# Scores of 64-wide heads in an encoder trunk: two products over 128 rows, then two over 64 rows each

## The chip, the cores and the metric

The kernel runs on one core of a Trainium2 chip. A core has TensorE (PE; its weight loads are listed apart as PEld), VectorE (DVE), ScalarE (ACT), GpSimd (POOL) and SyncE (SP), which issues most DMAs. The metric is the device time of one execution in microseconds.

## What is computed

Two layers of a bidirectional encoder over 1024 tokens of width 1024. In each layer one input projection feeds three kinds of attention, whose outputs are concatenated, projected and added; then comes a gated feed-forward. Cut to the attention scores:

```python
# MLA: 6 heads, 96 wide, 64-wide values
o_a = _dense_attention(q_a, k_a, v_a, MLA_QK ** -0.5, "bhqd,bhsd->bhqs", "bhqs,bhsv->bhqv")
# differential: 4 heads of two 64-wide score maps each
s = jnp.einsum("bhcqd,bhcsd->bhcqs", qb, k_b).astype(jnp.float32) * scale_b
p = jax.nn.softmax(s, axis=-1)
a = p[:, :, 0] - lam * p[:, :, 1]
# grouped-query: 6 query heads, 2 key heads, 64 wide
o_c = _dense_attention(q_c, k_c, v_c, GQA_DIM ** -0.5, "bkgqd,bksd->bkgqs", "bkgqs,bksv->bkgqv")
```

So a layer has 8 + 6 = 14 score maps of 64-wide heads and 6 of 96-wide heads, each of 1024 queries by 1024 keys.

## The kernel before

Every operand of a large product is held as two parts, a high one (the value rounded to fp32r) and a low one (what the rounding left). A product is then the sum of high by low, low by high and high by high. The parts of queries and keys are written to DRAM once (`qd`, `kd` for differential heads, `qg`, `kg` for grouped-query heads, `qm`, `km` for MLA), with the features along the rows, and read back by head.

The attention stage handles 320 calls of `soft` over both layers: 20 score maps, 8 blocks of 128 queries, 2 layers. One call makes the scores of 128 queries against all 1024 keys in a PSUM tile `sc` of two banks, 512 keys ("half") in each; VectorE takes the maximum over the tile (L688) and ScalarE the exponential (L689). The tile has two buffers. Then the probabilities are transposed on PE (`spread`, L704), split into high and low (L709, L710) and multiplied with the values (L890).

For a 64-wide head both parts of one operand fit on the 128 rows of a tile. `load_q` makes two query tiles, `q[0]` with high over low and `q[1]` with low over high. `load_k` makes one key tile for each half of the keys, `k[0]` and `k[1]`, both with high over low. Then `q[1]` by a key tile is low by high plus high by low, and `q[0]` by it is high by high plus low by low: two products of 128 rows for each half, four for a call. The 96-wide heads need three products for each half, six for a call.

What sets the order: `order` mixes the streams of units (five of single heads to two of differential ones), `front`, `one_spread` and `value_products` lay the work of several units between each other, and queries and keys are loaded two blocks of 256 queries ahead. The instructions are placed by a scheduler that works from a time line of its own, so that SP's row of DMAs can shift when PE's work changes.

`neg_lambda` (L179) has one small matmul of 64 rows in each layer, and the finish of a differential head has small ones of 128 rows (L811).

Of the kernel before, what the change touches and what calls it, by code (L numbers as in the profile page):

```python
# [20 lines left out]
P = 128  # L21
# [44 lines left out]
def encoder(ctx: ExitStack, tc: tile.TileContext, a: dict, out: bass.AP):  # L66
    nc = tc.nc
    ve, ac, po, pe, sy = nc.vector, nc.scalar, nc.gpsimd, nc.tensor, nc.sync
# [14 lines left out]
    def ps_s(name):  # L83
        return banks["pool"].tile([P, 2, 512], F32, tag="s", name=name)
# [12 lines left out]
    def ps_u(name):  # L97
        return banks["pool"].tile([P, 512], F32, tag="u", name=name)

    def ps_v(name):  # L100
        return banks["pool"].tile([P, 512], F32, tag="v", name=name, bufs=5)
# [94 lines left out]
    for l in range(L):  # L196
# [78 lines left out]
        def gain_row(name):  # L275
# [11 lines left out]
            lambda k, tt, i=i: XT[tt // 4][i][:, k, tt % 4 * P : (tt % 4 + 1) * P] for i in range(2)  # L287
# [343 lines left out]
        with tc.tile_pool(name=f"c{l}", bufs=2, side=there, reuse_waits="tile") as cp:  # L631
            QB = 256
            n = QB // P
            def stacked(t, parts, rows, cols):
                for r, src in enumerate(parts):
                    sy.dma_start(out=f(t[r * rows : (r + 1) * rows, :]), in_=src[:, cols])
                return t[: rows * len(parts)]

            def load_k(k, rows, tag):

                out = []
                for i in range(2):
                    orders = [[k[0], k[1]]] if 2 * rows <= P else [[k[0]], [k[1]]]
                    out.append(
                        [
                            stacked(
                                ops.tile([P, 512], F32R, tag=tag, name="k"), o, rows,
                                slice(i * 512, (i + 1) * 512),
                            )
                            for o in orders  # L650
                        ]
                    )
                return out
# [21 lines left out]
            def soft(q, k, i):  # L675
                ps = ps_s("sc")
                cut = slice(i * P, (i + 1) * P)
                for half, kk in enumerate(k):
                    products = ((1, 0), (0, 1), (0, 0)) if len(kk) == 2 else ((1, 0), (0, 0))
                    for at, (x, y) in enumerate(products):  # L680
                        pe.matmul(  # L681
                            ps[:, half, :], q[x][:, cut], kk[y], start=at == 0, stop=at == len(products) - 1
                        )
                nm = cp.tile([P, 1], F32, tag="nm", name="nm", bufs=6)
                s = cp.tile([P, 1], F32, tag="sum", name="sum", bufs=8)
                p = cp.tile([P, S], F32, tag="p", name="p", bufs=7)
                pf = ps.rearrange("p a b -> p (a b)")
                ve.tensor_reduce(nm, pf, axis=AX.X, op=ALU.max, negate=True)  # L688
                ac.activation(p, pf, AF.Exp, bias=nm, accum_out=s)  # L689
                return p, s  # L690
# [34 lines left out]
            class Single:  # L725
# [8 lines left out]
                def load(self):  # L734
                    self.kk = load_k(self.k, self.rows, "b")
                    (self.vv,) = v_tiles(self.v, "b", 2)
# [4 lines left out]
                def front(self, b, i):  # L741
                    p, s = soft(b.q, self.kk, i)
                    r = recip(s)
                    po.tensor_scalar(p, p, r, 1.0, ALU.mult, ALU.mult)  # L744
                    yield p
# [14 lines left out]
            class Diff:  # L760
# [5 lines left out]
                def load(self):  # L766
                    self.kk = [
                        load_k([kd[p, i] for p in range(2)], DD, "a") for i in (2 * self.h, 2 * self.h + 1)
                    ]
                    self.vv = [  # L770
                        t[:, k * 2 * P : (k + 1) * 2 * P].rearrange("p (c x) -> p c x", c=2)
                        for t in v_tiles(vd[self.h], "a", 3)
                        for k in range(TT // 2)
                    ]
# [7 lines left out]
                def front(self, b, i):  # L782

                    if i == 0:
                        b.es = cp.tile([P, QB // P], F32, tag="es", name="es")
                    p0, s0 = soft(b.q[0], self.kk[0], i)
                    yield None
                    p1, s1 = soft(b.q[1], self.kk[1], i)
                    r1 = recip(s1)
                    c = cp.tile([P, 1], F32, tag="c", name="c", bufs=6)  # L790
                    po.tensor_scalar(c, s0, nlam, 1.0, ALU.mult, ALU.mult)
                    po.tensor_scalar(b.es[:, i : i + 1], s0, s0, EPS, ALU.mult, ALU.mult)
                    po.tensor_scalar(p1, p1, c, r1, ALU.mult, ALU.mult)
                    po.tensor_tensor(out=p0, in0=p0, in1=p1, op=ALU.add)
                    yield p0
# [70 lines left out]
            fronts, lagging, spreads, products, ends = [], [], [], [], []  # L866
# [30 lines left out]
            at = 0  # L897
# [85 lines left out]
        for tt in range(TT):  # L983
            ps = ps_u("psd") if tt % 2 else ps_v("psd")
# [48 lines left out]
        for tt in range(TT):  # L1033
# [5 lines left out]
            ps = ps_u("psd") if tt % 2 else ps_v("psd")  # L1039
# [204 lines left out]
        at = 0  # L1244
        w_d = a["w_down"][l].rearrange("(n two p) d -> two p n d", two=2, p=P)
        for p0 in range(0, NP, NC):
# [49 lines left out]
            for step, (an, bn, bank, start, (row, c)) in enumerate(steps):  # L1296
# [7 lines left out]
                for tt in range(TT // 2):  # L1304
                    if start:
                        acc[bank, tt] = ps_u("psy") if bank == "c" and tt < 3 else ps_v("psy")
                    ps = acc[bank, tt]
# [3 lines left out]
                    x = XQ[row][c][:, tt, :]  # L1311
# [39 lines left out]
```

## Time and profile before

| | |
|---|---|
| median of 3 runs | 3335.84 us (3328.43 to 3336.86) |
| profiled execution | 3334.67 us |
| its span, first to last instruction | 3332.9 us |
| mean granted TensorE clock | 0.974 |
| scores L681: matmuls, first and last start | 1472, at 401.9 and 2535.9 us |
| maximum L688 on VectorE | 320 of 1213 ns |
| exponential L689 on ScalarE | 320 of 1120 ns |

The time of an execution is its span and what lies around it. Matmuls are pipelined: a matmul's listed duration includes a tail that lies under the next one, so that what a matmul costs is read from start to start. The busy shares are averages over stages with different limits; the attention stages are two of them, from about 401 to 880 us and from 2056 to 2540 us.

### The profile page before, as it was taken

What the parts mean: (1) busy time and instruction counts of PE and PEld (TensorE: products, weight loads), DVE (VectorE), ACT (ScalarE), POOL (GpSimd) and SP (SyncE); (2) the same over time, 40 slices, a digit from 0 to 9 for tenths busy, and PEclk for the clock granted to TensorE, in tenths of its full rate; (3) what the DMA queues carried; (4) which work ended last, traced back from release to release, by engine and by line L of the source; (5) the groups of instructions that cost most, each with busy time, mean ns of one, the idle gap of its engine ahead of it and who ended that gap; (6) DMA issues with size and microseconds to landing.
All of it is one profiled execution on the core that took longest, in us unless ns stands there. A gap on an engine that the chain in (4) does not pass through costs nothing.

```text
span 3332.9 us, 50137 instructions
## 1 busy us (share of the span) xinstructions
PE 3112.6 (93%) x17628; PEld 2725.3 (82%) x17628; DVE 2412.0 (72%) x4880; ACT 1589.5 (48%) x3010; POOL 1067.6 (32%) x1178
## 2 busy tenths in 40 slices
PE   8888899999898999989998888999898989999899
PEld 7888888888787888878898888888787878888787
DVE  5876688999637665667669776999995376666776
ACT  4433377777624333333344344777774243333332
POOL 1634466666302100100026344666663020101000
PEclk9999899999999999999998999999999999999999
DMA  5565634333572333374344665433336723334632
GB/s 150 158 197 164 192 100 118 109 97 98 166 260 81 101 114 95 101 258 152 98 138 144 187 189 177 117 106 111 90 102 205 233 79 95 101 108 142 230 133 98
DMA packets 386075, 466.16 MB, mean 140 GB/s; under 512 B 36768, under 2 KB 275360, under 8 KB 385824
## 3 DMA queue, kind: packets, MB, share of 16 engines
q1 hardware_dynamic: 372416, 418.38, 40.6%
q0 software_dynamic: 13408, 44.57, 4.0%
q8 instruction: 140, 2.29, 0.3%
q14 instruction: 111, 0.91, 0.1%
HBM read 313.42 MB, written 149.42 MB: 139 GB/s over the span
## 4 chain that ended last, share of the span: by engine, by line
PE 69%; DVE 19%; DMA 5%; issue 2%; ACT 2%; POOL 1%; SPq 1%; ACTq 0%; DVEq 0%; POOLq 0%
PE pv L890 6%; PE sc L681 6%; PE psa L157 5%; PE psa L158 5%; PE psa L159 5%; PE ptc L704 4%; PE psb L157 4%; PE psb L158 4%; PE psb L159 4%; PE psy L157 4%; PE psy L159 4%; PE psy L158 4%; DVE nm L688 4%; DVE pl L710 3%; PE psc L157 2%
## 5 line engine op out<-in xcount | busy, mean ns | idle before, releaser
L681 PE MATMUL sc<-k,q 128*128 128x512 f32 (+1 forms) x1472 | 421.5, 414 | 23.7 <-ACT p L689 23.0
L157 PE MATMUL psb<-wh,xl 128*128 128x256 f32 (+2 forms) x1280 | 389.2, 305 | 38.8 <-DVE vst L431 20.2
L688 DVE TENSOR_REDUCE nm<-sc 128x1 f32<-128x1024 f32 x320 | 388.1, 1213 | 46.3 <-PE sc L681 44.7
L689 ACT ACTIVATE p<-sc,nm 128x1024 f32<-128x1024 f32 x320 | 358.5, 1120 | 81.2 <-DVE nm L688 71.4
L158 PE MATMUL psb<-wl,xh 128*128 128x256 f32 (+2 forms) x1280 | 386.8, 302 | 2.7 <-POOL wl L124 2.2
L159 PE MATMUL psb<-wh,xh 128*128 128x256 f32 (+2 forms) x1280 | 385.2, 301 | 0.0
L710 DVE TENSOR_TENSOR pl<-ptc,ph 128x512 fp32r<-128x512 f32 x512 | 337.5, 677 | 14.1 <-ACT ph L709 13.3
L709 ACT CAST ph<-ptc 128x512 fp32r<-128x512 f32 x512 | 288.8, 586 | 105.7 <-PE ptc L704 99.9
L681 PEld LDWEIGHTS sc<-k,q 128*128 128x128 f32 (+1 forms) x1472 | 260.0, 192 | 70.1 <-ACT p L689 30.3
L890 PE MATMUL pv<-pl,v 128*128 128x256 f32 x1024 | 277.8, 296 | 39.2 <-DVE pl L710 27.7
L704 PE MATMUL ptc<-ident,p 128*128 128x128 f32 x2048 | 290.5, 276 | 19.1 <-DVE pl L710 15.5
L890 PE MATMUL pv<-ph,v 128*128 128x256 f32 x1280 | 304.3, 288 | 2.8 <-DVE ot L756 2.4
L157 PEld LDWEIGHTS psb<-wh,xl 128*128 128x128 f32 x1280 | 250.5, 196 | 43.0 <-issue 13.6
L704 PEld LDWEIGHTS ptc<-ident,p 128*128 128x128 f32 x2048 | 242.1, 143 | 52.6 <-DVE pl L710 10.3
L744 POOL TENSOR_SCALAR p<-p,rec 128x1024 f32<-128x1024 f32 x192 | 216.1, 1128 | 136.3 <-DVE rec L694 99.1
L157 PE MATMUL psy<-bh,al 128*128 128x512 f32 x616 | 241.9, 396 | 16.6 <-DVE al L124 16.6
L158 PEld LDWEIGHTS psb<-wl,xh 128*128 128x128 f32 x1280 | 251.1, 196 | 3.8 <-POOL wl L124 2.8
L1222 POOL DMA_DIRECT2D hd<-h x66 | 35.9, 545 | 681.0 <-DVE h L1163 434.3
L159 PEld LDWEIGHTS psb<-wh,xh 128*128 128x128 f32 x1280 | 250.3, 196 | 0.0
L158 PE MATMUL psy<-bl,ah 128*128 128x512 f32 x616 | 241.7, 392 | 0.1
L890 PEld LDWEIGHTS pv<-pl,v 128*128 128x128 f32 x1024 | 195.4, 191 | 56.0 <-DVE pl L710 37.4
L159 PE MATMUL psy<-bh,ah 128*128 128x512 f32 x616 | 241.2, 392 | 0.0
(220 smaller groups left out, 7656.2 us busy)
## 6 DMA issues: line engine op xcount, KB each, us to landing
graw<-in_w_gate_up SPq DMA_DIRECT2D x88, 512.0 KB, 5.3
ar<-hd SPq DMA_DIRECT2D x28, 1024.0 KB, 6.1
hd<-hs POOLq DMA_DIRECT2D x88, 256.0 KB, 3.0
hd<-h POOLq DMA_DIRECT2D x66, 256.0 KB, 2.4
q<-qd SPq DMA_DIRECT2D x256, 64.0 KB, 2.4
B<-od SPq DMA_DIRECT2D x12, 1280.0 KB, 7.6
wraw<-in_w_in SPq DMA_DIRECT2D x56, 256.0 KB, 3.2
o<-od SPq DMA_DIRECT2D x10, 1280.0 KB, 11.2
```

The lines of the kernel that those rows point to most:

```text
L157: pe.matmul(ps, xl, wh, start=first, stop=False, skip_group_check=more)
L158: pe.matmul(ps, xh, wl, start=False, stop=False, skip_group_check=more)
L159: pe.matmul(ps, xh, wh, start=False, stop=last, skip_group_check=more)
L681: pe.matmul(ps[:, half, :], q[x][:, cut], kk[y], start=at == 0, stop=at == len(products) - 1)
L688: ve.tensor_reduce(nm, pf, axis=AX.X, op=ALU.max, negate=True)
L689: ac.activation(p, pf, AF.Exp, bias=nm, accum_out=s)
L704: pe.transpose(pt[:, k * P : (k + 1) * P], p[:, (4 * b + k) * P : (4 * b + k + 1) * P], ident)
L709: ac.copy(h, pv)
L710: ve.tensor_tensor(out=pl[:, 4 * b : 4 * b + 4, i * P : (i + 1) * P], in0=pv, in1=f(h), op=ALU.subtract,)
L744: po.tensor_scalar(p, p, r, 1.0, ALU.mult, ALU.mult)
L890: pe.matmul(b.o, x, y, start=first, stop=last)
L1222: po.dma_start(out=HB[b][p], in_=src)
```

## The change

It concerns 64-wide heads alone. The key tile of the second half is now stacked with low over high. The first product of the first half is still `q[1]` by `k[0]` (low by high plus high by low); that of the second half becomes `q[0]` by `k[1]` (high by low plus low by high). Both run over all 128 rows. Then only high by high is left. For the first half it lies on rows 0 to 63 of `q[0]` and `k[0]`, for the second on rows 64 to 127 of `q[1]` and `k[1]`, and each is a product of 64 rows. The low by low product, which the 128-row form brought along for these heads, is no longer computed. The order of the four products becomes: first half, second half, first half, second half.

```diff
             def load_k(k, rows, tag):
 
+
                 out = []
                 for i in range(2):
-                    orders = [[k[0], k[1]]] if 2 * rows <= P else [[k[0]], [k[1]]]
+                    orders = [[k[i], k[1 - i]]] if 2 * rows <= P else [[k[0]], [k[1]]]
...
-                for half, kk in enumerate(k):
-                    products = ((1, 0), (0, 1), (0, 0)) if len(kk) == 2 else ((1, 0), (0, 0))
-                    for at, (x, y) in enumerate(products):
-                        pe.matmul(
-                            ps[:, half, :], q[x][:, cut], kk[y], start=at == 0, stop=at == len(products) - 1
-                        )
+                if len(k[0]) == 1:
+
+
+                    for half, (kk,) in enumerate(k):
+                        pe.matmul(ps[:, half, :], q[1 - half][:, cut], kk, start=True, stop=False)
+                    for half, (kk,) in enumerate(k):
+                        rows = slice(half * 64, half * 64 + 64)
+                        pe.matmul(ps[:, half, :], q[half][rows, cut], kk[rows], start=False, stop=True)
+                else:
+                    for half, kk in enumerate(k):
+                        products = ((1, 0), (0, 1), (0, 0))
+                        for at, (x, y) in enumerate(products):
+                            pe.matmul(ps[:, half, :], q[x][:, cut], kk[y], start=at == 0, stop=at == 2)
```

PE's order in layer 0, well inside the attention stage: transposes of probabilities (`ptc`), scores of a 64-wide head, transposes, scores of a 96-wide head, values (`pv`). Before:

```order
L704 MATMUL ptc<-ident,p 128x128 x4
L681 MATMUL sc<-k,q 128x512 x4
L704 MATMUL ptc<-ident,p 128x128 x8
L681 MATMUL sc<-k,q 128x512 x6
L890 MATMUL pv<-ph,v 128x256 x2
```

The same place in the changed kernel, whose lines stand two to eight further down:

```order
L712 MATMUL ptc<-ident,p 128x128 x4
L683 MATMUL sc<-k,q 128x512 x2
L686 MATMUL sc<-k,q 128x512 x2
L712 MATMUL ptc<-ident,p 128x128 x8
L691 MATMUL sc<-k,q 128x512 x6
L898 MATMUL pv<-ph,v 128x256 x2
```

The four score products have become two of 128 rows (L683) and, right behind, two of 64 rows (L686); the row shows the output's size, which is the same. The 96-wide head's six and all around them stand where they stood.

PE's order at the start of the first attention stage, with the semaphores that an instruction waits for (those named DMA are loads of queries and keys, DVE and Activation the release of a PSUM buffer). Before:

```order
L681 MATMUL sc<-k,q 128x512 [waits DMAHW5_49,DMAHW4_49,DMAHW7_49,DMAHW0_49,DVE_49]
L681 MATMUL sc<-k,q 128x512 [waits DMAHW6_49]
L681 MATMUL sc<-k,q 128x512 [waits DMAHW1_49,DMAHW0_49]
L681 MATMUL sc<-k,q 128x512
L681 MATMUL sc<-k,q 128x512 [waits DMAHW3_49,DMAHW2_49,DVE_49]
```

In the changed kernel:

```order
L683 MATMUL sc<-k,q 128x512 [waits DMAHW5_49,DMAHW4_49,DMAHW7_49,DMAHW0_49,DVE_49]
L683 MATMUL sc<-k,q 128x512 [waits DMAHW6_49,DMAHW1_49,DMAHW0_49]
L686 MATMUL sc<-k,q 128x512 x2
L683 MATMUL sc<-k,q 128x512 [waits DMAHW3_49,DMAHW2_49,DVE_49]
L683 MATMUL sc<-k,q 128x512 [waits DMAHW2_49]
```

The loads of the second key tile are waited for by the second product of a call instead of the third; the two products of 64 rows wait for nothing of their own.

SP's order in layer 0 where it differs: loads of queries (`q<-qd`, `q<-qm`) and keys (`k<-kd`) and stores of outputs (`od<-ohl`). Before:

```order
L636 DMA k<-kd 64x512
L636 DMA q<-qd 64x256 x6
L720 DMA od<-ohl 128x2x256
L636 DMA q<-qd 64x256 x2
L720 DMA od<-ohl 64x2x256
L671 DMA v<-vm 128x1024
L636 DMA q<-qm 96x256 x2
L636 DMA k<-kd 64x512 x7
```

In the changed kernel:

```order
L636 DMA q<-qd 64x256 x7
L728 DMA od<-ohl 128x2x256
L636 DMA q<-qd 64x256
L728 DMA od<-ohl 64x2x256
L672 DMA v<-vm 128x1024
L636 DMA q<-qm 96x256 x2
L636 DMA k<-kd 64x512 x8
```

One load of keys has moved behind the queries ahead of it. VectorE's, ScalarE's and GpSimd's rows are the same in both kernels but for line numbers.

## The prediction

> **What bounds the kernel now.** I read the page first, then the two stretches in which scores are computed, then the chain of waits inside them, then single instructions. The page, with the span, the engines and the chain that ended last:
>
> ```profile
> span 3332.9 us, 50137 instructions
> PE 3112.6 (93%) x17628; PEld 2725.3 (82%) x17628; DVE 2412.0 (72%) x4880; ACT 1589.5 (48%) x3010; POOL 1067.6 (32%) x1178
> PE 69%; DVE 19%; DMA 5%; issue 2%; ACT 2%; POOL 1%; SPq 1%; ACTq 0%; DVEq 0%; POOLq 0%
> ```
>
> PE carries the kernel as a whole, but the change touches only the attention stage of each layer. The first scores of layer 0 start at 401 us, the last of layer 1 at 2536 us; the two stages as windows (columns: engine busy times, PE clock, DMA share, GB/s):
>
> ```profile
> core 0: us, PE busy (x) PEld busy (x) DVE busy (x) ACT busy (x) POOL busy (x), PEclk, DMA share, GB/s
> 401.00:880.00 479.00, 442.57 (x2908) 391.40 (x2907) 428.22 (x802) 357.58 (x702) 291.62 (x314) 0.98 0.39 115
> 2056.00:2540.00 484.00, 443.62 (x2934) 391.41 (x2932) 434.09 (x812) 363.68 (x714) 293.79 (x316) 0.99 0.40 116
> ```
>
> PE is busy 92% of such a stage and VectorE 89%. So there are two engines near their limits, and a microsecond on PE is worth less than a microsecond at the end. How much less is read from the chain of work inside each window, and from who waits:
>
> ```profile
> by line: PE sc L681 22.1%; PE pv L890 21.6%; PE ptc L704 13.1%; DVE nm L688 13.0%; DVE pl L710 10.0%; DVE t L137 3.2%; DVE r L138 2.6%; DVE t L136 2.1%; ACT p L689 1.8%; issue 1.7%; DMA raw<-in_w_o 1.3%; DVE ot L756 1.2%; PE pb L827 1.0%; D
> by line: PE sc L681 21.4%; PE pv L890 20.8%; PE ptc L704 13.2%; DVE nm L688 12.6%; DVE pl L710 9.9%; DVE t L137 3.2%; DVE r L138 2.5%; issue 2.4%; ACT p L689 2.3%; DVE t L136 2.1%; DMA raw<-in_w_o 1.4%; DVE ot L756 1.2%; ACT ph L709 1.0%; P
> ...
> DVE nm L688 <- PE sc L681: 23.9, 32, 2.6
> PEld pv L890 <- DVE pl L710: 18.8, 18, 2.7
> PEld sc L681 <- ACT p L689: 14.3, 13, 4.1
> ```
>
> The score products (L681) hold 22.1% of 479 us and 21.4% of 484 us, 106 + 104 = 210 us, of both chains. In layer 0 VectorE stands 23.9 us for scores, and PE stands for VectorE and ScalarE about as long. Neither engine has the stage to itself.
>
> **What a block of scores costs now.** A block is one call of `soft`: 128 queries against 1024 keys. For 64-wide heads it is four products of 128 rows by 512 columns. The counts by shape, and one block with the instructions around it (start, length of the group):
>
> ```profile
> L681 PE MATMUL sc<-k,q 128*128 128x512 f32 x896 | 265.3, 419 | 17.6 <-ACT p L689 17.3
> ...
> 708.98 0.28 PE L890 MATMUL pv<-ph,v 128*128 128x256 f32 x1
> 709.10 1.09 PE L681 MATMUL sc<-k,q 128*128 128x512 f32 x4
> 710.03 0.49 PE L704 MATMUL ptc<-ident,p 128*128 128x128 f32 x3
> ```
>
> The listed mean of 419 ns includes the tail of a pipelined matmul; what counts is start to start: 710.03 - 709.10 = 0.93 us for four, 0.2325 us each. 896 / 4 = 224 blocks are changed; the other 96 blocks, of the 96-row heads, have six products each (320 blocks in all) and stay. All score products take (896 + 576) x 0.2325 = 342 us, of which 210 us lie on the chain: 0.61. That is the share of a saved score microsecond that reaches the end; for a lengthening it is the lower bound, 1.0 the upper.
>
> **What the change removes.** Two of the four 128-row products become two 64-row products, on rows 0-63 and 64-127, each with 512 columns and into its own PSUM bank. If these two run side by side they take one slot instead of two: -0.2325 us a block, 224 x 0.2325 = -52 us on PE. The number of matmuls and weight loads stays; only their rows fall.
>
> **What it adds.** Each block now goes from 128-row to 64-row matmuls and back. The trace of before has exactly two such visits, one in each layer: L179, two small matmuls with 64 rows in the middle of a stream of 128-row products. PE rows of the first and its weight loads, then the second:
>
> ```profile
> 65.78 0.28 PE L159 MATMUL psb<-wh,xh 128*128 128x256 f32 x1
> 65.90 0.28 PE L157 MATMUL psb<-wh,xl 128*128 128x256 f32 x1
> 66.11 0.38 PE L179 MATMUL pl__5271<-lp,ones 64*128 64x2 f32 x2
> 66.42 0.38 PE L158 MATMUL psb<-wl,xh 128*128 128x256 f32 x1
> 66.64 0.28 PE L159 MATMUL psb<-wh,xh 128*128 128x256 f32 x1
> ...
> 65.66 0.19 PEld L159 LDWEIGHTS psb<-wh,xh 128*128 128x128 f32 x1
> 65.78 0.19 PEld L157 LDWEIGHTS psb<-wh,xl 128*128 128x128 f32 x1
> 66.10 0.29 PEld L179 LDWEIGHTS pl__5271<-lp,ones 64*128 64x128 f32 x2
> 66.41 0.19 PEld L158 LDWEIGHTS psb<-wl,xh 128*128 128x128 f32 x1
> ...
> 1725.31 0.28 PE L157 MATMUL psb<-wh,xl 128*128 128x256 f32 x1
> 1725.52 0.38 PE L179 MATMUL pl__22793<-lp,ones 64*128 64x2 f32 x2
> 1725.83 0.39 PE L158 MATMUL psb<-wl,xh 128*128 128x256 f32 x1
> 1726.05 0.28 PE L159 MATMUL psb<-wh,xh 128*128 128x256 f32 x1
> ```
>
> In the plain stream a load stands one matmul ahead (the load at 65.78 belongs to the matmul at 65.90). Around L179 that stops: its load starts at 66.10, 0.01 us ahead of its own matmul, and so does the next load back, at 66.41. Both layers give the same gaps within 0.01 us and the profile names no wait there, so I read it as the price of the visit and not of late data. For comparison, two equally small matmuls of all 128 rows (L811):
>
> ```profile
> 706.26 0.28 PE L890 MATMUL pv<-ph,v 128*128 128x256 f32 x1
> 706.38 0.28 PE L811 MATMUL pm<-ones,osq 128*128 128x1 f32 x2
> 706.52 1.19 PE L681 MATMUL sc<-k,q 128*128 128x512 f32 x4
> 707.54 0.28 PE L811 MATMUL pm<-ones,osq 128*128 128x1 f32 x2
> ...
> 706.26 0.31 PEld L811 LDWEIGHTS pm<-ones,osq 128*128 128x128 f32 x2
> 706.49 0.77 PEld L681 LDWEIGHTS sc<-k,q 128*128 128x128 f32 x4
> ```
>
> Here the loads run ahead as always. The visit's price, term by term:
> - going in: 66.11 - 65.90 = 0.21 us instead of 706.38 - 706.26 = 0.12: +0.09
> - the pair and going out: 66.42 - 66.11 = 0.31 us instead of 706.52 - 706.38 = 0.14: +0.17
> - the first full product after it, whose load lies open: 66.64 - 66.42 = 0.22 us instead of 0.12: +0.10. After L811 the four scores take 707.54 - 706.52 = 1.02 us instead of 0.93, +0.09 as well, so this term may belong to the small pair and not to the change of rows.
>
> So a visit costs 0.26 us without the last term and 0.36 us with it. I take 0.36: before, the load behind a block was hidden, and after it the row of L179 shows it open. There is one more unknown: whether the loads of the two halves go beside each other. Two loads of L179 take 0.29 us where one takes 0.19, so a second load can put the second half 0.10 us behind the first; L179's two share their rows, the new pair doesn't, so I count it at nothing and keep 0.10 us for the upper end.
>
> **The sum.** Per block 0.36 - 0.2325 = +0.13 us (bounds: 0.26 - 0.2325 = +0.03 and 0.46 - 0.2325 = +0.23). Times 224: +29 us of PE time (+7 to +51). The end gets 0.61 to 1.0 of it; PE grows into more of the chain as it slows, but its present waits for VectorE absorb some, so I take 0.8: +23 us. On the profiled execution's 3334.67 us (its span of 3332.9 and 1.8 around it; the median of the runs is 3335.84) this is **3358 us**; this case's own range is 3334.67 + 0.61 x 7 = 3339 to 3334.67 + 51 = 3386.
>
> On this place the Trainium skill speaks against the change: TensorEngine Tiling (Array Packing), section Key Properties, says that a change of the tiling mode, as opposed to a change of tile within it, drains the TensorE. The trace agrees, with the 0.20 us from the last full matmul's start at 65.90 to the load at 66.10.
>
> **What costs nothing.** The second key tile is now stacked low over high. It is loaded by the same DMAs, and a handful of them change places by a row or two in SP's queue:
>
> ```profile
> q<-qd SPq DMA_DIRECT2D x256, 64.0 KB, 2.4
> k<-kd SPq DMA_DIRECT2D x64, 128.0 KB, 3.7
> ```
>
> They are issued two blocks of 256 queries ahead, that is at least four units of a stage that takes 479 / 160 = 3 us a unit of `soft`; 12 us cover 3.7. Were that cover gone, each of the 28 loads of keys could cost its 3.7 us, but none of PE's waits above is for keys. Each half's first product now comes second in the block instead of third, so the second tile is wanted 0.23 us earlier, well inside the same cover. VectorE, ScalarE and GpSimd keep their instructions and order. No wait is added; the reduction behind a block (L688) sees both halves end together instead of one after the other, but it waited for the last of them before too.
>
> **Rivals.**
> 1. *The pair is side by side and the visit is nearly free* (faster). The pause around L179 would then belong to its small plain-float matmuls and not to 64 rows. All of -52 us is saved on PE, 0.61 of it at the end: -32 us, 3303 us. VectorE allows it: its 428 us of a 479 us stage leave 51 us. It decides wherever a visit costs under 0.2325 us a block. For it: only two visits are on record, both with two columns. Against it: L811 is as small and as plain and shows no pause going in.
>    In the Trainium skill, TensorE: Matmul & The Clock Gate, section Measured speedup vs the span model, counts packed row tiles as one matmul and about 4 ns for each further tile. By that rule a block is three slots, which is this rival; no run here shows a packed pair yet.
> 2. *The two halves don't overlap* (slower still). A block keeps four slots and pays 0.26 to 0.36 us: 58 to 81 us on PE, at 0.8 46 to 65 us, 3381 to 3399 us. For it: no matmul in this trace overlaps another by more than its tail. Against it: different rows and different PSUM banks. This is also the case that the change doesn't do what its words say.
> 3. *It cancels.* A visit of 0.19 to 0.27 us eats the saved slot, within about 0.04 us x 224 = 9 us: 3335 us, give or take 9.
>
> **How the numbers follow.** Forecast 0.45, rival 1 0.24, rival 2 0.12, rival 3 0.19. A measurement of this kernel can tell about 0.3%, 10 us, from no change. Slower: 0.42 of the forecast, 0.12, and 0.02 of rival 3, together 0.56. Within: 0.03 of the forecast, 0.02 of rival 1, 0.15 of rival 3, 0.20. Faster: 0.22 of rival 1 and 0.02 of rival 3, 0.24. The range from 3308 to 3392 leaves out the far end of rival 1 (about 0.1) and the upper half of rival 2 (0.06); the likeliest case alone spans 3339 to 3386.
>
> **What would show it.** In the profile after, the load of the first 64-row product should start about 0.3 us (a 0.21 us stream and 0.09) behind the start of the last 128-row one and not beside it; the two 64-row matmuls should start within 0.1 us of each other; from a block's first product to the next instruction should be 1.0 to 1.1 us instead of 0.93, and each stage some 11 us longer. If the 64-row loads stand ahead as the others do, rival 1 is right; if the second half starts 0.23 us behind the first, rival 2. The forecast is also wrong if blocks lengthen as worked out but the stages don't: then PE's waits for VectorE took it up.

## The result, and the profile after

The changed kernel takes 3354.70 us in the median of 5 runs (3350.54 to 3357.92), the kernel before 3335.84 us (3328.43 to 3339.32). The ratio is 1.0056, with a 95% interval from 1.0041 to 1.0072: slower by about 19 us. The forecast was 3358 us.

The page of the changed kernel; its profiled execution took 3357.92 us, the longest of the five:

```profile
span 3356.1 us, 50132 instructions
PE 3146.6 (94%) x17628; PEld 2673.6 (80%) x17628; DVE 2417.7 (72%) x4880; ACT 1593.2 (47%) x3010; POOL 1069.6 (32%) x1178
PE 72%; DVE 17%; DMA 5%; ACT 2%; issue 2%; SPq 1%; POOL 0%; ACTq 0%; DVEq 0%; POOLq 0%
```

PE has 34 us more of busy time with the same 17628 matmuls, and its share of the chain that ended last rose from 69% to 72%, at VectorE's cost. Where the time lies is seen from the first score and the last transpose of each layer. The answers by line, for layer 0 and layer 1 (duration in ns as min/median/max, then first and last start in us); first the kernel before:

```profile
L681 PE MATMUL sc<-k,q x736: 387/395/794, 401.9 to 882.2; 128*128 128x512 f32 x112, 96*128 96x512 f32 x72
L704 PE MATMUL ptc<-ident,p x1024: 270/272/421, 411.1 to 894.9; 128*128 128x128 f32 x171
...
L681 PE MATMUL sc<-k,q x736: 387/394/792, 2056.6 to 2535.9; 128*128 128x512 f32 x112, 96*128 96x512 f32 x72
L704 PE MATMUL ptc<-ident,p x1024: 270/272/448, 2067.4 to 2548.6; 128*128 128x128 f32 x171
```

The same of the changed kernel (its transposes are L712):

```profile
L683 PE MATMUL sc<-k,q x224: 387/397/795, 398.6 to 856.3; 128*128 128x512 f32 x112
L712 PE MATMUL ptc<-ident,p x1024: 270/273/477, 407.9 to 903.2; 128*128 128x128 f32 x171
...
L683 PE MATMUL sc<-k,q x224: 387/398/796, 2063.1 to 2524.0; 128*128 128x512 f32 x112
L712 PE MATMUL ptc<-ident,p x1024: 270/273/472, 2074.0 to 2571.8; 128*128 128x128 f32 x171
```

From the first score to the last transpose, layer 0 takes 903.2 - 398.6 = 504.6 us instead of 493.0, layer 1 508.7 instead of 492.0: +28 us together. The stage of layer 0 begins 3 us earlier and the stretch between the stages is 2 us shorter; behind the last transpose both kernels take 784.3 us. All of the loss is in the two attention stages.

The granted clock of these stages is lower too. It is TensorE's clock as a share of its full speed, here a mix of stretches at 1 and at 0.5; at 0.5 a score matmul is listed with up to 796 ns where the median is 398. The two stages of the changed kernel as windows (columns as in the prediction, the clock third from the end):

```profile
401.00:880.00 479.00, 446.00 (x2835) 354.93 (x2836) 422.52 (x788) 351.72 (x689) 286.11 (x308) 0.97 0.38 112
2056.00:2540.00 484.00, 452.48 (x2874) 358.80 (x2873) 420.38 (x782) 350.04 (x686) 282.88 (x304) 0.97 0.40 115
```

The kernel before had 0.98 and 0.99. Over the whole span the mean of the five runs is 0.972, against 0.976 in the eleven runs of the kernel before beside the first experiments: an estimate of 0.004 x 3355 = 13 us less of full clock.

One block of the changed kernel, at the place that the prediction showed of before (PE, then its weight loads; start and length of the group):

```profile
709.72 0.28 PE L898 MATMUL pv<-ph,v 128*128 128x256 f32 x1
709.84 0.63 PE L683 MATMUL sc<-k,q 128*128 128x512 f32 x2
710.40 0.50 PE L686 MATMUL sc<-k,q 64*128 64x512 f32 x2
710.82 0.66 PE L712 MATMUL ptc<-ident,p 128*128 128x128 f32 x4
711.32 0.60 PE L835 MATMUL pb<-dg,ones 128*128 128x256 f32 x2
...
709.72 0.31 PEld L683 LDWEIGHTS sc<-k,q 128*128 128x128 f32 x2
710.39 0.18 PEld L686 LDWEIGHTS sc<-k,q 64*128 64x128 f32 x2 [0.37 <-issue]
```

Three things are to be seen. The two 64-row matmuls, 0.494 us each by their median, take 0.50 us together, so they start together and do run side by side. Their two loads take 0.18 us together, where two loads into the same rows took 0.29: the loads go side by side too. But the load starts at 710.39, 0.55 us behind the first full product, instead of ahead of its matmul: PE's loads stood idle for 0.37 us, and the profile names nobody ("issue") as the one waited for.

The same over all blocks: the 64-row matmuls' durations, then groups by shape (count, then busy time and mean, then idle time just before):

```profile
L686 PE MATMUL sc<-k,q x448: 491/494/794, 399.1 to 2524.3; 64*128 64x512 f32 x150
...
L683 PE MATMUL sc<-k,q 128*128 128x512 f32 x448 | 161.1, 442 | 15.3 <-ACT p L697 15.3
L686 PE MATMUL sc<-k,q 64*128 64x512 f32 x448 | 114.8, 509 | 0.0
L686 PEld LDWEIGHTS sc<-k,q 64*128 64x128 f32 x448 | 42.7, 187 | 85.0 <-issue 85.0
```

224 pairs have 85.0 us of such idle time ahead of their loads, 0.38 us each. A matmul of 0.509 us mean is listed 448 times, but its busy time is 114.8 us, 0.51 for each pair: half of them lie beside the other half everywhere.

### The profile page after: what moved, and what is told of

Its sections match the earlier page's. It is cut to its first block, busy times and chain, and to the rows that moved or that the text cites. A ratio compares the mean times of both kernels' runs of the same rounds, so it can differ in the third digit from the quotient of the medians.

```text
span 3356.1 us, 50132 instructions
## 1 busy us (share of the span) xinstructions
PE 3146.6 (94%) x17628; PEld 2673.6 (80%) x17628; DVE 2417.7 (72%) x4880; ACT 1593.2 (47%) x3010; POOL 1069.6 (32%) x1178
## 4 chain that ended last, share of the span: by engine, by line
PE 72%; DVE 17%; DMA 5%; ACT 2%; issue 2%; SPq 1%; POOL 0%; ACTq 0%; DVEq 0%; POOLq 0%
PE pv L898 7%; PE psa L157 5%; PE psa L158 5%; PE psa L159 5%; PE ptc L712 5%; PE psb L157 4%; PE psb L158 4%; PE psb L159 4%; PE psy L157 4%; PE psy L159 4%; PE psy L158 4%; DVE nm L696 3%; DVE pl L718 3%; PE sc L691 3%; PE psc L157 2%; PE psc L158 2%
## 5 line engine op out<-in xcount | busy, mean ns | idle before, releaser
L898 PE MATMUL pv<-pl,v 128*128 128x256 f32 x1024 | 285.3, 303 | 35.6 <-DVE pl L718 25.5
L712 PE MATMUL ptc<-ident,p 128*128 128x128 f32 x2048 | 301.2, 283 | 14.2 <-DVE pl L718 11.6
L898 PE MATMUL pv<-ph,v 128*128 128x256 f32 x1280 | 312.0, 294 | 1.7 <-DVE ot L764 1.4
L712 PEld LDWEIGHTS ptc<-ident,p 128*128 128x128 f32 x2048 | 239.2, 145 | 56.2 <-issue 26.3
L898 PEld LDWEIGHTS pv<-ph,v 128*128 128x128 f32 x1280 | 235.3, 194 | 12.6 <-issue 7.2
L123 ACT CAST wh<-ws 128x512 fp32r<-128x512 f32 x176 | 108.6, 623 | 266.5 <-PE psa L159 235.4
```

What stands on the lines that cost most here:

```text
L123: (hi_eng or ac.copy)(h, src)
L712: pe.transpose(pt[:, k * P : (k + 1) * P], p[:, (4 * b + k) * P : (4 * b + k + 1) * P], ident)
L898: pe.matmul(b.o, x, y, start=first, stop=last)
```

## The experiments

All were timed over five rounds beside the kernel before (3331 to 3334 us in those series); a ratio is to it, with its 95% interval. They vary two things: the slots of 512 columns a block (0.2325 us each) and the visits to 64 rows.

**Three 128-row products, no visit.**

```diff
-                        pe.matmul(ps[:, half, :], q[1 - half][:, cut], kk, start=True, stop=False)
-                    for half, (kk,) in enumerate(k):
-                        rows = slice(half * 64, half * 64 + 64)
-                        pe.matmul(ps[:, half, :], q[half][rows, cut], kk[rows], start=False, stop=True)
+                        pe.matmul(ps[:, half, :], q[1 - half][:, cut], kk, start=True, stop=half == 1)
+                    pe.matmul(ps[:, 0, :], q[0][:, cut], k[0][0], start=False, stop=True)
```

> Keys stacked as in the changed kernel, both mixed products, then high by high of the first half alone as a 128-row product (that of the second half is left out): three slots of 0.2325 us a block, and no visit to 64 rows. Theory V (the price is the visit, two changes of row count a block): without it one slot a block is saved, 224 x 0.2325 = 52 us on PE, 0.6 to 0.7 of it at the end: 32 to 36 us under the kernel before, about 3300 to 3304 us. Theory O (the time comes from the new order of products, from both halves ending together, or from the moved key loads, and not from 64 rows): this kernel has all of that too and stays above 3336 us.

3315.38 us, ratio 0.9952 (0.9939 to 0.9965). It is faster than before, so theory O, by which it would have stayed above 3336 us, falls. On PE nothing of the new stacking and order shows: over all blocks at full clock that end in transposes, the median from a block's first product to the next instruction falls from 1.01 to 0.78 us, by just a slot. But 16 us is half of what theory V expected. This is what the change would have given if the visit were free.

**One visit, nothing side by side.**

```diff
-                    orders = [[k[i], k[1 - i]]] if 2 * rows <= P else [[k[0]], [k[1]]]
+                    orders = [[k[0], k[1]]] if 2 * rows <= P else [[k[0]], [k[1]]]
...
-                        pe.matmul(ps[:, half, :], q[1 - half][:, cut], kk, start=True, stop=False)
+                        pe.matmul(ps[:, half, :], q[1][:, cut], kk, start=True, stop=False)
...
-                        rows = slice(half * 64, half * 64 + 64)
-                        pe.matmul(ps[:, half, :], q[half][rows, cut], kk[rows], start=False, stop=True)
+                        pe.matmul(ps[:, half, :], q[0][:64, cut], kk[:64], start=False, stop=True)
```

> As the changed kernel, but both 64-row products lie on rows 0 to 63 (both key tiles high over low, as before): one visit a block, and no side by side. Theory V with side by side in the changed kernel: a block is four slots and one visit of about 0.34 us, 224 x 0.34 = 76 us on PE, at 0.7 53 us above the kernel before, about 3389 us; the two 64-row products start about 0.21 us apart. Theory S (the halves of the changed kernel don't really overlap, whatever the profile's starts say): the same time as the changed kernel, 3355 us.

3379.59 us, ratio 1.0141 (1.0124 to 1.0159): 47 us above the kernel before, where the changed kernel lies 19 above it, so theory S falls. A block of it, with its loads:

```profile
699.89 0.63 PE L683 MATMUL sc<-k,q 128*128 128x512 f32 x2
700.45 0.72 PE L685 MATMUL sc<-k,q 64*128 64x512 f32 x2
701.10 1.09 PE L711 MATMUL ptc<-ident,p 128*128 128x128 f32 x8
...
699.77 0.31 PEld L683 LDWEIGHTS sc<-k,q 128*128 128x128 f32 x2
700.45 0.29 PEld L685 LDWEIGHTS sc<-k,q 64*128 64x128 f32 x2 [0.37 <-issue]
701.10 0.86 PEld L711 LDWEIGHTS ptc<-ident,p 128*128 128x128 f32 x8 [0.36 <-issue]
```

Four slots and one visit take 701.10 - 699.89 = 1.21 us, against 0.93 us of the same four slots without a visit: +0.28 us, and the transposes behind find their load unprepared (0.36 us of idle time). The pair takes 0.72 us instead of 0.50, 0.22 us more: a slot.

**Two visits.**

```diff
                     for half, (kk,) in enumerate(k):
                         pe.matmul(ps[:, half, :], q[1 - half][:, cut], kk, start=True, stop=False)
-                    for half, (kk,) in enumerate(k):
                         rows = slice(half * 64, half * 64 + 64)
```

> As the changed kernel, but each half's 64-row product comes right behind its mixed product: two visits a block, four slots, nothing side by side. Theory V: 2 x 0.34 = 0.68 us a block more than before, 152 us on PE, at 0.7 to 0.8 106 to 122 us, about 3442 to 3458 us. Theory F (a fixed price a block, for instance the new stacking or the open load behind the block, however often rows change): about 3389 us, as with one visit.

3462.88 us, ratio 1.0386 (1.0372 to 1.0400), a little above theory V's range and far from theory F's. A block:

```profile
705.49 0.39 PE L683 MATMUL sc<-k,q 128*128 128x512 f32 x1
705.81 0.49 PE L685 MATMUL sc<-k,q 64*128 64x512 f32 x1
706.23 0.50 PE L683 MATMUL sc<-k,q 128*128 128x512 f32 x1
706.66 0.50 PE L685 MATMUL sc<-k,q 64*128 64x512 f32 x1
707.09 1.09 PE L711 MATMUL ptc<-ident,p 128*128 128x128 f32 x8
```

Each change of row count stands in a row by itself: 0.32 us to the first 64-row product (0.09 over a slot), then 0.42, 0.43 and 0.43 us from each product to the next (0.19 to 0.20 over). Four slots and two visits take 1.60 us, 0.67 us more than 0.93. With 0.06 us for the transposes behind, as in the changed kernel (shown further down), that is 0.73 us, 0.36 us a visit; with one visit it is 0.28 + 0.06 = 0.34 us.

**The second 64-row product left out.**

```diff
-                        pe.matmul(ps[:, half, :], q[1 - half][:, cut], kk, start=True, stop=False)
-                    for half, (kk,) in enumerate(k):
-                        rows = slice(half * 64, half * 64 + 64)
-                        pe.matmul(ps[:, half, :], q[half][rows, cut], kk[rows], start=False, stop=True)
+                        pe.matmul(ps[:, half, :], q[1 - half][:, cut], kk, start=True, stop=half == 1)
+                    pe.matmul(ps[:, 0, :], q[0][:64, cut], k[0][0][:64], start=False, stop=True)
```

> As the changed kernel, but high by high of the second half is left out: one visit a block with a single 64-row product. Theory V with side by side: the second product was free, so the time is that of the changed kernel, about 3355 us, and 50 us above the kernel with three 128-row products, which differs by the visit alone. Theory S (no overlap): a 0.21 us slot a block less, 48 us on PE and 30 us at the end, about 3322 us.

3349.95 us, ratio 1.0052 (1.0037 to 1.0066), against the changed kernel's 1.0056: the second product is free. Against the first experiment, from which it differs by the rows of one product alone, it is slower by 35 us; theory V had said 50, because it took that kernel to be faster than it was. The mean clocks of the two are 0.972 and 0.971, so this pair shows the price of the visits by itself: 35 us at the end, of 224 x 0.34 = 76 us on PE.

**Two products left out.** Why did a saved slot give 16 us and not 32? The next run saves another.

```diff
-                    for half, (kk,) in enumerate(k):
-                        pe.matmul(ps[:, half, :], q[1 - half][:, cut], kk, start=True, stop=False)
-                    for half, (kk,) in enumerate(k):
-                        rows = slice(half * 64, half * 64 + 64)
-                        pe.matmul(ps[:, half, :], q[half][rows, cut], kk[rows], start=False, stop=True)
+                    for half, (kk,) in enumerate(k):
+                        pe.matmul(ps[:, half, :], q[1 - half][:, cut], kk, start=True, stop=True)
```

> Both high by high products of the 64-wide heads are left out: two slots a block, no visit, 104 us less on PE than the kernel before; against three slots and no visit (3315 us), 52 us less. Theory D (VectorE is the limit behind PE, so that little of what PE saves in this stage reaches the end): well under half of the second 52 us comes out, 3298 to 3310 us. Theory P (a fixed share of what PE saves reaches the end, the 0.61 of the prediction or the third that the first slot gave): by 0.61 3283 us, by a third 3298 us.

3316.15 us, ratio 0.9942 (0.9931 to 0.9954), where three products had 0.9952 (0.9939 to 0.9965): of the second 52 us at most a few came out. Theory P falls. Theory D fits, more strongly than it was put. The chain of waits in its stage of layer 0, and the busy times there:

```profile
by line: DVE nm L693 19.5%; PE pv L895 18.0%; DVE pl L715 15.4%; PE ptc L709 9.3%; PE sc L688 6.1%; PE sc L683 4.7%; DVE t L136 4.5%; issue 3.2%; DVE r L138 2.9%; DVE t L137 2.8%; ACT p L694 1.9%; DVE ot L761 1.5%; DVE r L133 1.0%; DVE rec 
...
401.00:880.00 479.00, 416.83 (x2766) 361.55 (x2766) 444.78 (x823) 370.04 (x728) 297.71 (x321) 0.96 0.40 117
```

VectorE's maximum (L693) now leads the chain with 19.5%, where it had 13.0% in the kernel before, and VectorE is busy 444.8 of 479 us.

VectorE need not have taken all of it. The clock in this stage is 0.96, and with three products it is 0.96 too, where the kernel before had 0.98:

```profile
401.00:880.00 479.00, 432.69 (x2832) 381.63 (x2830) 434.50 (x810) 362.70 (x712) 293.40 (x317) 0.96 0.39 117
```

Over all their runs the mean clock is 0.976 before, 0.971 with three products and 0.968 with two, by estimate 17 and 23 us less of full clock. The first is as much as the 16 us that theory V missed. In the traces the lower clock goes with a PE that waits more: well inside the two stages the kernel before has six stretches at half clock, the kernel with three products 17, and each starts behind 3.4 us in which PE was busy for at most 53% by its listed durations. How the missing time is shared between VectorE's waits and the clock that falls with them isn't shown, for no run holds the clock.

**A visit shared by two blocks.** A control first: in the differential heads the mixed products of both score maps come first, then all high by high ones, all over 128 rows. Then the same with 64-row pairs for those heads, one visit for two maps. `mixed` and `highs` are the two loops of products in `soft`, `exps` is what follows them. In both kernels `issue_after` keeps the high by high products behind, and the grouped-query heads keep four 128-row products.

```diff
-                    p0, s0 = soft(b.q[0], self.kk[0], i)
+                    maps = [mixed(b.q[m], self.kk[m], i) for m in range(2)]
+                    with tc.issue_after(maps[1][1].ins):
+                        for m in range(2):
+                            highs(maps[m][0], b.q[m], self.kk[m], i)
+                    p0, s0 = exps(maps[0][0])
                     yield None
-                    p1, s1 = soft(b.q[1], self.kk[1], i)
+                    p1, s1 = exps(maps[1][0])
```

> A control: four 128-row products a block as in the kernel before, no visit, but in the differential heads the mixed products of both score maps come first and then all four high by high ones together, so that both buffers of the score tile are held longer. If holding them costs nothing: the time of the kernel before, 3332 to 3336 us. If VectorE and ScalarE run dry meanwhile: up to one maximum of 1.2 us for each of the 64 pairs, 77 us, more.

> As the control, but the four high by high products of a differential pair are 64-row products, two by two side by side: one visit for two blocks (64 visits), two slots saved for each; the grouped-query heads keep four 128-row products. Theory V (a price for each visit, whatever it serves): 64 x (0.34 - 2 x 0.2325) = -8 us on PE against the control, 3 to 6 us less at the end, so that a shared visit pays. Theory F (a price for each block that uses 64 rows): 128 x 0.11 = +14 us on PE, 9 us above the control.

The control takes 3412.03 us, ratio 1.0237 (1.0222 to 1.0251): holding both score buffers costs 79 us, the full price that was allowed for. The shared visit takes 3402.92 us, 1.0204 (1.0190 to 1.0217), 9 us less than its control, so that a visit that saves two slots pays, as theory V says. The size isn't explained: 3 to 6 us were expected, and the price on PE was only 8. The order is no use, for what it holds up is worth more. Its four products in one visit:

```profile
709.59 0.70 PE L680 MATMUL sc<-k,q 128*128 128x512 f32 x2
710.23 0.72 PE L687 MATMUL sc<-k,q 64*128 64x512 f32 x4
710.88 1.53 PE L726 MATMUL ptc<-ident,p 128*128 128x128 f32 x12
```

From the four's start to the next instruction 0.65 us, against 0.42 us for a pair: one slot more.

**VectorE made lighter.** The finish of a differential head refines an inverse root in three Newton steps of three small instructions on VectorE. With two steps left out in that place:

```diff
-    def newton(pool, v, n, tag):
+    def newton(pool, v, n, tag, steps=3):
...
-        for _ in range(3):
+        for _ in range(steps):
...
-                    r = newton(cp, v, n, "o")
+                    r = newton(cp, v, n, "o", 1)
```

It was given to the kernel before, the kernel with three 128-row products and the changed kernel; a fourth run leaves only one step out of the kernel before:

> The kernel before, with one Newton step instead of three behind the differential heads (two steps of refining an inverse root are left out): VectorE loses 2 x 1.23 us in each of 32 finishes, 78 us in all. Theory D (VectorE limits the stage beside PE): a part reaches the end, about a third to two thirds, 25 to 50 us less, 3283 to 3308 us. Theory P (PE alone limits): no change, 3333 us.

> The kernel with three 128-row products a block and no visit (high by high of the second half left out), with the same lighter finish. Theory D: with VectorE relieved the missing slot (52 us on PE) is worth more than the 17 us that it gave at full VectorE load: 28 to 45 us under the one-step kernel before. Theory P (a fixed share of a third reaches the end): again about 17 us under it.

> The changed kernel with the same lighter finish. Theory D: PE is now the one limit, so that the visit's net 0.11 us a block, 25 us on PE, passes nearly whole: 21 to 28 us above the one-step kernel before. Theory P: the same 19 us as without the lighter finish.

> The kernel before with two Newton steps instead of three (one step of refining is left out): VectorE loses 39 us in all. Theory D: about half of what the one-step kernel gains, 12 to 25 us less, 3308 to 3321 us. Theory P: no change.

| kernel | three steps | one step |
|---|---|---|
| before | 3332.21 us | 3292.31 us, 0.9873 (0.9860 to 0.9887) |
| three 128-row products, no visit | 3315.38 us, 0.9952 (0.9939 to 0.9965) | 3264.52 us, 0.9790 (0.9777 to 0.9803) |
| changed | 3354.70 us, 1.0056 (1.0041 to 1.0072) | 3310.34 us, 0.9928 (0.9915 to 0.9941) |

Each ratio is to the kernel before in its own series. With two steps the kernel before takes 3322.44 us, 0.9965 (0.9953 to 0.9976), 10 us less, short of the 12 to 25 expected. With one step VectorE's busy time falls by 62 us (2412.0 to 2350.1 us on the two pages; 78 were expected), and 40 us reach the end although PE is the busier engine, as theory D says; the mean clock rises from 0.975 to 0.979. With VectorE lighter the saved slot gives 28 us instead of 16, at the low end of what theory D expected, and again the clock falls with it, from 0.979 to 0.974. The visit costs the changed kernel 18 us over its one-step neighbour, not the 21 to 28 us expected: that part stays at what it was, as theory P had it.

**A version that beats both.** Nothing is left out; the three steps go to GpSimd.

```diff
+            if pooled:
+                po.tensor_tensor(out=t, in0=r, in1=r, op=ALU.mult)
+                po.tensor_tensor(out=t, in0=t, in1=h, op=ALU.mult)
+                po.tensor_scalar(t, t, 1.5, 1.0, ALU.add, ALU.mult)
+                po.tensor_tensor(out=r, in0=r, in1=t, op=ALU.mult)
+                continue
...
-                    r = newton(cp, v, n, "o")
+                    r = newton(cp, v, n, "o", True)
```

> The kernel before with the three Newton steps of the differential heads' finish on GpSimd instead of VectorE, nothing left out: VectorE loses 9 instructions of 0.41 us, 3.7 us in each of 32 finishes, 118 us in all, and GpSimd, busy 292 of 479 us in a stage, gets 12 of about 0.27 us. Theory D: at least what two steps fewer gave, 40 us, since VectorE is relieved by more: 3275 to 3295 us. Rival: GpSimd's queue, which also scales the probabilities, holds these up by 3.2 us a finish and eats the gain: 3310 to 3336 us.

3261.30 us, ratio 0.9791 (0.9774 to 0.9809), 69 us under the kernel before and better than expected; VectorE's busy time falls by 99 us (2412.0 to 2313.1). Its stage of layer 0 (busy times of PE, loads, VectorE, ScalarE, GpSimd) and the chain there:

```profile
401.00:880.00 479.00, 462.08 (x3075) 409.98 (x3074) 396.55 (x683) 370.65 (x731) 334.73 (x515) 0.99 0.43 127
...
by line: PE sc L687 28.0%; PE pv L896 26.1%; PE ptc L710 17.5%; DVE nm L694 5.4%; DVE pl L716 4.0%; ACT p L695 3.4%; issue 2.5%; ACT ph L715 1.8%; PE psd L163 1.1%; DMA raw<-in_w_o 1.1%; PE psd L164 1.1%; PE psd L165 1.1%; PE pb L833 1.1%; 
```

PE is busy 462 of the same 479 us, with 3075 matmuls in them instead of 2908, and its scores, values and transposes hold 72% of the chain instead of 57%; the clock is 0.99. By these readings a saved score slot would be worth most in this kernel; that wasn't run.

## Why the prediction was right, point by point

- **The visit's price.** The forecast was 0.09 going in, 0.17 for the pair and going out and 0.10 for the open load behind, 0.36 us in all. In the changed kernel going in costs 710.40 - 709.84 - 2 x 0.2325 = 0.095 us; the pair and going out 710.82 - 710.40 - 0.2325 = 0.19 us; and the transposes behind take 711.32 - 710.82 = 0.50 us instead of 0.44 in the row of before that follows: +0.06. Together 0.34 us.

```profile
710.03 0.60 PE L704 MATMUL ptc<-ident,p 128*128 128x128 f32 x4
710.47 0.38 PE L827 MATMUL pb<-dg,ones 128*128 128x256 f32 x1
```

  The open load was the term that was most in doubt (the first bound left it out); it is there, smaller than forecast. The kernels with one and two visits of four slots give 0.34 and 0.36 us. All this is read from single blocks, and the 0.93 us of the block of before is a short one; over all blocks at full clock with transposes behind, the median goes from 1.01 to 1.07 us, and four transposes behind a block from 0.36 to 0.41 us. The difference is the same 0.11 us. The forecast's sign of 1.0 to 1.1 us is met by this median, while the block shown has 0.98.
- **The slot saved.** The forecast took the pair to lie side by side, with loads beside each other. Both hold, in the rows and by the product left out, which moved nothing. Rival 2, at 0.12, is what the same-rows kernel shows: 3380 us, just under the rival's 3381 to 3399.
- **The sum.** +0.13 us a block was forecast, 0.34 - 0.2325 = +0.11 us is measured: 25 us on PE instead of 29.
- **The share that reaches the end.** 0.8 was taken, 19 / 25 = 0.76 measured; with one visit and four slots 47 of 76 us, 0.62; with two visits 130 of 163 us, 0.80. That 0.8 came so near is in part luck. The share isn't one number: between the kernel with three full products and the one with a half-height third it is 35 / 76 = 0.46, under the 0.61 that the forecast took for the lower bound. And the sum has no term for the clock, which granted some 13 us less; what of the 19 us is due to it isn't shown.
- **Rival 1 was mis-sized.** It put a free pair at 0.61 x 52 = 32 us less; the kernel with three 128-row products gives 16, and two slots saved give hardly more than one. Its argument that VectorE's 428 us in a stage of 479 leave 51 us failed: with two slots saved VectorE is busy 444.8 of 479 us, leads the chain, and yields almost nothing further. And it put at nothing the clock, which falls as PE waits more, 0.976 to 0.971 for the first slot. That the stage could only gain half of it makes the change worse than it looked: the best case was 16 us, for a visit to be had for nothing.
- **What costs nothing.** No cost of it shows: the same stacking, order of halves and loads stand in the kernel with three products, whose blocks are shorter on PE by just a slot, and in neither stage does PE wait for a load of keys. A cost elsewhere, within the 16 us that are missing there, isn't excluded; no run has the new order with four full products.

The rule on draining that the Trainium skill gives in TensorEngine Tiling (Array Packing), section Key Properties, agrees with the traces, which have 0.37 us of idle loads at each visit. The span model that the Trainium skill gives in TensorE: Matmul & The Clock Gate, section Measured speedup vs the span model, holds inside a visit (0.50 us for two of 0.494) and leaves out the way in and out.

That it is a drain of the array, and no other pause of its sequencer, was not shown: the records show when loads and matmuls start, not why they stand.

## What to carry to other kernels

Packing two half-height matmuls side by side saves what it says, one slot, but a stream of full-height matmuls pays 0.34 us for each visit, one and a half slots of 512 columns here. One saved slot a visit didn't pay, two did. Before cutting work from the busiest engine, cut the same from its neighbour in a run or two: here 52 us off PE gave 16 and a second 52 next to nothing, while moving small instructions off VectorE, the less busy engine, gave 69. The chain's share of 0.61 was no fixed price: a third of the first slot came out, and 0.46 to 0.80 of what visits added. Look at the granted clock of the stage beside the busy times, for it fell where PE waited more.

## What the runs showed of the hardware that was not expected

By their means, instructions on 128 x 2 elements look dearer on VectorE than on GpSimd. The Newton steps on VectorE in the kernel before, and on GpSimd in the last kernel (count, busy us, mean ns):

```profile
L137 DVE TENSOR_TENSOR t<-t,h 128x2 f32<-128x2 f32 x120 | 53.8, 448 | 1.3
L138 DVE SCALAR_TENSOR_TENSOR r<-t,r 128x2 f32<-128x2 f32 x120 | 42.4, 353 | 1.0
L136 DVE TENSOR_TENSOR t<-r 128x2 f32<-128x2 f32 x120 | 33.4, 278 | 1.4
...
L139 POOL TENSOR_SCALAR t<-t 128x2 f32<-128x2 f32 x96 | 20.0, 208 | 6.5
L138 POOL TENSOR_TENSOR t<-t,h 128x2 f32<-128x2 f32 x96 | 19.2, 200 | 5.3
```

The means mislead. Behind the stage of layer 0, where GpSimd does nothing meanwhile, the same instructions take 0.16 us each on VectorE, and a step 973.39 - 972.80 = 0.59 us from start to start; on GpSimd a step, with one instruction more, took 618.56 - 617.46 = 1.10 us. Inside a stage some take far longer. First three of the kernel before behind the stage, then two inside it, then what GpSimd did at those two times:

```profile
972.80 0.16 DVE L136 TENSOR_TENSOR t<-r 128x2 f32<-128x2 f32 x1
973.00 0.16 DVE L137 TENSOR_TENSOR t<-t,h 128x2 f32<-128x2 f32 x1
973.20 0.16 DVE L138 SCALAR_TENSOR_TENSOR r<-t,r 128x2 f32<-128x2 f32 x1
...
532.21 1.36 DVE L136 TENSOR_TENSOR t<-r 128x2 f32<-128x2 f32 x1
550.40 0.90 DVE L137 TENSOR_TENSOR t<-t,h 128x2 f32<-128x2 f32 x1
...
531.16 2.39 POOL L794 TENSOR_TENSOR p<-p 128x1024 f32<-128x1024 f32 x1
550.18 1.12 POOL L744 TENSOR_SCALAR p<-p,rec 128x1024 f32<-128x1024 f32 x1 [0.71 <-DVE r L133]
```

Both long ones end with GpSimd's instruction, at 533.57 and 533.55 us and at 551.30 us. So do all: of the 288 Newton instructions in the two stages, 90 take over 0.25 us, and each of these ends within 0.03 us of the end of a GpSimd instruction. The 288 take 118 us; at 0.15 us each it would be 43, so some 75 us of VectorE's busy time is spent until GpSimd has finished. This is the likely reason why the steps were worth moving, though GpSimd is the slower engine for them. No run takes the wait away and leaves the steps on VectorE, so that part is argued.
